# Stationary low parts in four pieces at hashed positions, one load buffer less

## The chip, the cores and the metric

The kernel runs on one core of one Trainium2 chip. The metric is the time of one execution on the device in microseconds (us). A core has TensorE (matmuls, PE in the profile, with its weight loads as PEld), VectorE (DVE), ScalarE (ACT), GpSimd (POOL) and SyncE (SP, which issues most transfers), each with its own queue that is worked off in order, and 128 partitions of on-chip memory.

## The reference

A decoder trunk of two layers on 256 tokens with 2048 channels, all in float32. The first layer is a Mamba-2 mixer, the second attends to keys and values that are computed once from the stream after the first layer. After each mixer stands a gated MLP with a short causal convolution, and after each of the four sub-layers a layer norm of the weighted residual:

```python
for layer in range(DEPTH):
    if layer < N_A_LAYERS:
        mix = mamba2_mixer(h, ...)
    else:
        mix = moba_cross_attention(h, attn_w_q[j], attn_w_o[j], k_blk, v_blk, k_mean)
    h = layer_norm(DEEPNORM_ALPHA * h + mix, ln_mix_g[layer], ln_mix_b[layer])
    ffn = conv_ffn(h, ffn_w_up[layer], ffn_conv_w[layer], ffn_conv_b[layer], ffn_w_down[layer])
    h = layer_norm(DEEPNORM_ALPHA * h + ffn, ln_ffn_g[layer], ln_ffn_b[layer])
```

Nearly all the work lies in the products with the weights: `mamba_w_in`, `mamba_w_out`, `ffn_w_up`, `ffn_w_down`, `w_kv`, `attn_w_q`, `attn_w_o`, some 462 MB as they are cut (881 x 128 x 1024 x 4 bytes).

## The kernel before

A float32 number is written as a high part, rounded to the type float32r that TensorE takes, and a low part, the rest. A product of two numbers is then high x high + low x high + high x low. The activations of a sub-layer lie in on-chip memory once, high and low side by side, with the 2048 channels in 16 blocks k of 128: `hT[:, k, 0, :]` and `hT[:, k, 1, :]`, 256 tokens each (`gT`, `yT` and `aT` in the same form).

The weights are cut into 881 steps of 128 partitions x 1024 numbers (`chunks`, `cut`). For each step `load` issues one transfer of 512 KB into a buffer `raw` on SP's queue; `split` lets ScalarE copy it to `hi` in the type float32r (L209) and VectorE write `lo` = raw - hi (L210), and calls `load` for a step further on. `raw` has `RAW` buffers, `hi` and `lo` have four each, and `splits` keeps the splits up to four steps ahead of the products. A transfer waits on SP until its buffer is free, that is until the subtraction that read it last is done, and everything behind it on SP's queue waits with it: the parts of x and the small columns at the start, the residuals and gains of the norms (`fetch`, `fetch_gb`).

There are two kinds of product. In the 560 steps of mode "W" the weights are stationary and the activations moving; a step holds four blocks k of 256 output channels, thus 8 stationary blocks of 128 x 128 in `hi` and 8 in `lo`. `some` (called by `whole`) multiplies those of `hi` with both parts of the activations, 512 columns (L266), and those of `lo` with the high part, 256 columns (L269). The order of parts alternates, so that `hi` and `lo` stand in runs: in most mamba chunks runs of 16 matmuls of each kind, in the other chunks ("paired", two steps at a time) runs of 32. In the 320 steps of mode "X" the activations are stationary and the weights moving, six matmuls of 512 columns for each half of the tokens (`half`, L231, L232, L236); the last steps of the last chunk of a down projection do the second half in two pieces of 256 columns, into `tp` or `acc`.

Where `lo` lies is set by hand. In a line of 256 bytes (`LINE` is 64 numbers) the activations, `raw` and `hi` all begin at the same place. A tile `gap` of 48 numbers stands between `hi` and `lo`. In a W step the two halves of `lo` begin at the start of the tile and 8.5 lines on; in an X step `lo` begins 16 numbers into it:

```python
l = wts.tile([P, 2 * NC + LINE], F32R, tag="lo", name="lo")
if steps[i][0].mode == "W":
    l = l.rearrange("p (a n) -> p a n", a=2)[:, :, :NC]
else:
    l = l[:, LINE // 4:LINE // 4 + 2 * NC].rearrange("p (a n) -> p a n", a=2)
```

Counted from the beginning of the activations, a W step's low halves thus lie at 192 and 64 bytes in a line, and an X step's low part at 0.

The order of everything else (convolutions, the scan, attention, norms) is written out by hand against step numbers with `at`, `amid`, `within` and `beyond`.

Of the kernel before, what the change touches and what calls it, by code (L numbers as in the profile page):

```python
# [18 lines left out]
F32 = mybir.dt.float32  # L19
F32R = mybir.dt.float32r  # L20
# [4 lines left out]
P = 128  # L25
D = 2048
S = 256
# [12 lines left out]
NC = 512  # L40
HC = NC // 2
NEG = -1.0e30
LINE = 64
# [6 lines left out]
    N_COL += _n // P  # L50

LA = 3
RAW = 4
WARM0 = 18
HEAD, TAIL = 3, 4
LAST = 8
# [3 lines left out]
def chunks():  # L60

    z, b, c, dt = 0, 2 * DI, 2 * DI + NG * DS, 2 * DI + 2 * NG * DS

    def some(mode, name, layer, c0, n, nk):
        return [(mode, name, layer, c0 + i * NC, nk, False) for i in range(n)]

    def ffn(layer):
        up = [some(m, "ffn_w_up", layer, c + j * NC, 1, KD)[0] for j in range(DFF // NC)
              for m, c in (("W" if j else "X", 0), ("W", DFF))]
        return up + some("X", "ffn_w_down", layer, 0, 4, KF)  # L70

    out = some("W", "mamba_w_in", 0, b, 2, KD)
    out[0] = out[0][:5] + (True,)
    out += some("H", "mamba_w_in", 0, dt, 1, KD) + some("W", "mamba_w_in", 0, c, 2, KD)
    for g in range(NG):
        out += some("W", "mamba_w_in", 0, DI + g * NC, 1, KD) + some("W", "mamba_w_in", 0, z + g * NC, 1, KD)
    out += some("X", "mamba_w_out", 0, 0, 4, DI // P) + ffn(0)
    out += some("X", "w_kv", None, D, 1, KD) + some("W", "w_kv", None, 0, 4, KD) + some("W", "attn_w_q", 0, 0, 4, KD)
    return out + some("X", "w_kv", None, D + NC, 3, KD) + some("X", "attn_w_o", 0, 0, 4, KD) + ffn(1)
# [12 lines left out]
def yoco_kernel(ctx: ExitStack, tc: tile.TileContext, x, lmg, lmb, lfg, lfb, x_t, columns, w, out):  # L92
    nc = tc.nc
    base = ctx.enter_context(tc.tile_pool(name="base", bufs=1))
    wts = ctx.enter_context(tc.tile_pool(name="wts", bufs=LA + 1))
# [30 lines left out]
    steps, plan = [], chunks()  # L126
# [39 lines left out]
    raw_t, hi_t, lo_t = {}, {}, {}  # L166
# [5 lines left out]
    def load():  # L172
        i = pos["load"]
        if i >= n_steps:
            return
        pos["load"] += 1
        t = wts.tile([P, 2, NC], F32, tag="raw", name="raw", bufs=RAW)
        for e in (slice(0, 1), slice(1, 2)) if i == 0 else (slice(0, 2),):
            nc.sync.dma_start(t[:, e], w[i][:, e])
        raw_t[i] = t  # L180

    def split():
        i = pos["split"]
        pos["split"] += 1
        t = raw_t.pop(i)
        if i in spare:
            h, l = (bufs["h"][:, k:k + 2].rearrange("p k a t -> p k (a t)") for k in (spare[i], spare[i] + 2))
        else:
            h = wts.tile([P, 2, NC], F32R, tag="hi", name="hi")
            if not gap:  # L190
                gap.append(wts.tile([P, LINE * 3 // 4], F32R, tag="gap", name="gap", bufs=1))
            l = wts.tile([P, 2 * NC + LINE], F32R, tag="lo", name="lo")
            if len(gap) < 2:
                gap.append(wts.tile([P, LINE // 4], F32R, tag="gap2", name="gap2", bufs=1))
            if steps[i][0].mode == "W":
                l = l.rearrange("p (a n) -> p a n", a=2)[:, :, :NC]
            else:
                l = l[:, LINE // 4:LINE // 4 + 2 * NC].rearrange("p (a n) -> p a n", a=2)
        hi_t[i], lo_t[i] = h, l
        if steps[i][0].mode == "H":  # L200
            for a, w in enumerate((h, l)):
                v = t[:, a].rearrange("p (k n) -> p k n", k=8)
                w = w.rearrange("p a (k e n) -> p (a k) e n", e=2, n=NC // 8)
                nc.scalar.copy(w[:, :, 0], v)
                nc.vector.tensor_sub(w[:, :, 1], v, w[:, :, 0].bitcast(F32))
            return load()
        for e in ((0,), (1,)) if i < 2 else ((0, 1),):
            sl = slice(e[0], e[-1] + 1)
            nc.scalar.copy(h[:, sl], t[:, sl])  # L209
            nc.vector.tensor_sub(l[:, sl], t[:, sl], h[:, sl].bitcast(F32))  # L210
        load()

    def splits(i, most=2):

        for _ in range(1 if steps[i][0] in calm else most):
            j = pos["split"]
            ahead = LA + 1 + sum(i <= k < j for k in spare)
            if j < min(i + ahead, n_steps) and (j in spare or sum(k not in spare for k in hi_t) < LA + 1):
                split()
# [30 lines left out]
    def some(ch, s, p):  # L250

        i = ch.first + s
        nj = ch.nj
        w = ((hi_t, lo_t)[p][i]).rearrange("p a (k n) -> p a k n", n=nj * P)
        k0, half = ch.place(s)
        banks = [p[:, j, :] for p in ch.part[half:] for j in range(2)]
        first = ch.kinds(s)[0] == p
        for kk in range(ch.per):
            k = k0 + kk
            a, b = divmod(kk, ch.per // 2)  # L260
            begins, ends = first and k == 0, not first and k == ch.nk - 1
            for j in range(nj):
                yield
                js = slice(j * P, (j + 1) * P)
                if p == 0:
                    nc.tensor.matmul(banks[j], w[:, a, b, js], ch.x.both(k), start=begins, stop=ends,  # L266
                                     skip_group_check=True)
                else:
                    nc.tensor.matmul(banks[j][:, :S], w[:, a, b, js], ch.x.hi(k), start=begins, stop=ends,  # L269
                                     skip_group_check=True)  # L270

    def beside(i):
# [10 lines left out]
    def whole(i):  # L283

        ch, s = steps[i]
        if ch.mode == "H":
            return beside(i)
        a, b = ch.kinds(s)
        if not ch.paired:
            order = [(s, a), (s, b)]  # L290
        elif s % 2 == 0:
            order = [(s, a), (s + 1, a)]
        else:
            order = [(s - 1, b), (s, b)]
        late = ch.paired and s % 2
        n = len(order) * ch.per * ch.nj
        c = 0
        for t, p in order:
            for _ in some(ch, t, p):
                if c == (n // 2 if late else n * 3 // 8):  # L300
                    if late:
                        done(i - 1)
                    run(mid, i)
                    splits(i)
                c += 1
        if not ch.paired or late:
            done(i)
# [821 lines left out]
    for h in range(HEADS):  # L1129
        i, j = divmod(h, 4)  # L1130
# [87 lines left out]
```

## Time and profile before

| | |
|---|---|
| median of 2 runs | 2523.05 us (2522.97 to 2523.14) |
| the profiled execution | 2522.57 us |
| its span, first to last instruction | 2520.3 us |
| granted TensorE clock | 0.999 |
| ScalarE busy | 1365.8 us (54%) |
| VectorE busy | 1658.3 us (66%) |
| transfers of weights from issue to landing, median | 3.9 us |
| HBM read | 491.77 MB, 198 GB/s over the span with what is written |

The lines of the profile name the engine, the line of the program, the operation, what is written and read with the tiles' names, and how often; then busy time in us and the mean of one in ns, and the idle time of the engine before them with what ended it. In the timeline a row has the start and the length in us, and a count where neighbours are merged. A matmul's length there is its latency; successive matmuls overlap, so that the distance of starts is their pace.

### The profile page before, as it was taken

The page shows a single profiled execution, that of the slowest core. Times are in us where ns is not written, and L with a number is a line of the kernel's source. Part 1 is how long each engine was busy: PE and PEld are TensorE (multiplying, and loading weights), DVE is VectorE, ACT ScalarE, POOL GpSimd, SP SyncE. Part 2 cuts the span into 40 slices and gives each one's busy share as a digit, 9 for nine tenths or more (in the row PEclk, how much of TensorE's full clock was granted, in tenths as well). Part 3 has the DMA queues.
Part 4 walks back from the last instruction along what each step waited for, and adds up shares of the span by engine and source line. Part 5 has one row for each costly group of instructions (what it writes and reads, how often), then busy time and mean ns, then how long its engine had stood idle before and what let it go on. Part 6 is the DMA issues. An engine that isn't in the chain of part 4 may idle for free.

```text
span 2520.3 us, 36085 instructions
## 1 busy us (share of the span) xinstructions
PE 2507.3 (99%) x13983; PEld 2180.6 (87%) x13983; DVE 1658.3 (66%) x2140; ACT 1365.8 (54%) x1790; POOL 76.5 (3%) x96
## 2 busy tenths in 40 slices
PE   9999999999999999999999999999999999999998
PEld 8888888888888888888888888888888888888887
DVE  7878878755666766676445646645767676765545
ACT  6677787643465555554333445543556555554333
POOL 0000000000200000000000200000200000000001
PEclk9999999999999999999999999999999999999999
DMA  7656665666665565556676665456655665566674
GB/s 258 206 188 199 210 193 187 198 208 225 207 209 188 193 192 190 193 187 203 203 233 204 210 197 170 160 179 225 222 192 195 193 192 195 184 197 207 196 227 162
DMA packets 141739, 502.59 MB, mean 199 GB/s; under 512 B 15856, under 2 KB 16368, under 8 KB 141568
## 3 DMA queue, kind: packets, MB, share of 16 engines
q1 hardware_dynamic: 136448, 482.92, 58.9%
q0 software_dynamic: 4832, 16.85, 2.1%
q8 instruction: 109, 1.79, 0.3%
q14 instruction: 62, 0.51, 0.1%
q10 hardware_dynamic: 288, 0.52, 0.1%
HBM read 491.77 MB, written 8.45 MB: 198 GB/s over the span
## 4 chain that ended last, share of the span: by engine, by line
PE 99%; DMA 0%; DVE 0%; SPq 0%; issue 0%; ACT 0%
PE acc L266 40%; PE acc L269 21%; PE acc L231 11%; PE acc L232 11%; PE acc L236 11%; PE acc L804 1%; PE tp L406 0%; PE tp L236 0%; PE tp L232 0%; PE tp L231 0%; PE tp L813 0%; PE acc L787 0%; PE tp L1083 0%; PE tp L1117 0%; DMA raw<-in_w 0%; PE tp L1109 0%
## 5 line engine op out<-in xcount | busy, mean ns | idle before, releaser
L210 DVE TENSOR_TENSOR lo<-raw,hi 128x1024 fp32r<-128x1024 f32 (+1 forms) x869 | 1060.0, 1225 | 728.1 <-ACT hi L209 601.3
L209 ACT CAST hi<-raw 128x1024 fp32r<-128x1024 f32 (+1 forms) x869 | 908.9, 1048 | 833.1 <-PE acc L236 367.0
L266 PE MATMUL acc<-hT,hi 128*128 128x512 f32 x4480 | 1058.3, 391 | 1.4 <-DVE hT L569 1.2
L266 PEld LDWEIGHTS acc<-hT,hi 128*128 128x128 f32 x4480 | 826.4, 188 | 165.9 <-ACT hi L209 1.8
L269 PEld LDWEIGHTS acc<-hT,lo 128*128 128x128 f32 x4480 | 548.5, 188 | 15.5 <-issue 1.2
L269 PE MATMUL acc<-hT,lo 128*128 128x256 f32 x4480 | 555.0, 279 | 0.0
L232 PE MATMUL acc<-lo,gT 128*128 128x512 f32 (+1 forms) x678 | 254.5, 378 | 0.0
L231 PE MATMUL acc<-hi,gT 128*128 128x512 f32 (+1 forms) x678 | 254.1, 377 | 0.0
L236 PE MATMUL acc<-hi,gT 128*128 128x512 f32 (+1 forms) x678 | 200.8, 377 | 0.0
L232 PEld LDWEIGHTS acc<-lo,gT 128*128 128x128 f32 x678 | 127.6, 188 | 23.4
L231 PEld LDWEIGHTS acc<-hi,gT 128*128 128x128 f32 x678 | 127.6, 188 | 23.1
L236 PEld LDWEIGHTS acc<-hi,gT 128*128 128x128 f32 x678 | 124.9, 188 | 23.6
L232 PE MATMUL acc<-lo,yT 128*128 128x512 f32 (+1 forms) x270 | 98.6, 369 | 0.0
L231 PE MATMUL acc<-hi,yT 128*128 128x512 f32 (+1 forms) x270 | 98.5, 369 | 0.0
L231 PE MATMUL acc<-hi,hT 128*128 128x512 f32 x192 | 78.7, 410 | 0.0
L236 PE MATMUL acc<-hi,yT 128*128 128x512 f32 (+1 forms) x270 | 77.6, 369 | 0.0
L232 PE MATMUL acc<-lo,hT 128*128 128x512 f32 x192 | 75.4, 393 | 0.0
L636 DVE SCALAR_TENSOR_TENSOR g<-u,cols,g 128x254 f32<-128x254 f32 (+1 forms) x176 | 73.3, 478 | 2.8 <-ACT g L631 2.8
L609 DVE TENSOR_TENSOR u<-u,acc 128x512 f32<-128x512 f32 x108 | 73.5, 681 | 2.3 <-ACT u L608 1.4
L1033 ACT CAST gT<-v 128x512 fp32r<-128x512 f32 x44 | 27.3, 620 | 84.5 <-DVE v L1032 84.5
L636 DVE SCALAR_TENSOR_TENSOR v<-u,cols,v 128x254 f32<-128x254 f32 (+1 forms) x176 | 73.0, 477 | 0.0
L468 POOL TENSOR_TENSOR rs<-rs,mhalf 128x1 f32<-128x1 f32 x8 | 7.4, 931 | 1988.3 <-DVE nb L469 1988.3
(223 smaller groups left out, 1911.2 us busy)
## 6 DMA issues: line engine op xcount, KB each, us to landing
raw<-in_w SPq DMA_DIRECT2D x880, 512.0 KB, 3.9
mA<-acum_d POOLq DMA_DIRECT2D x16, 512.0 KB, 6.4
hres<-r POOLq DMA_DIRECT2D x12, 512.0 KB, 6.7
r<-hres SPq DMA_DIRECT2D x12, 512.0 KB, 4.4
eA<-acum_d POOLq DMA_DIRECT2D x16, 128.0 KB, 7.7
r<-in_x SPq DMA_DIRECT2D x4, 512.0 KB, 5.1
gb<-in_ln_mix_g SPq DMA_DIRECT2D x8, 256.0 KB, 5.3
gb<-in_ln_mix_b SPq DMA_DIRECT2D x8, 256.0 KB, 5.6
```

The source lines that it names most:

```text
L209: nc.scalar.copy(h[:, sl], t[:, sl])
L210: nc.vector.tensor_sub(l[:, sl], t[:, sl], h[:, sl].bitcast(F32))
L231: nc.tensor.matmul(a, th, h[:, kk, sl], start=k == 0, stop=False)
L232: nc.tensor.matmul(a, th, l[:, kk, sl], start=False, stop=False)
L236: nc.tensor.matmul(a, ch.x.lo(k)[:, ts], h[:, kk, sl], start=False, stop=k == ch.nk - 1)
L266: nc.tensor.matmul(banks[j], w[:, a, b, js], ch.x.both(k), start=begins, stop=ends, skip_group_check=True)
L269: nc.tensor.matmul(banks[j][:, :S], w[:, a, b, js], ch.x.hi(k), start=begins, stop=ends, skip_group_check=True)
L468: nc.gpsimd.tensor_tensor(self.rs[:, h, :], self.rs[:, h, :], mhalf[:, 0, :], op=OP.pow)
L609: nc.vector.tensor_add(dst, dst, p[:, :, :S])
L636: nc.vector.scalar_tensor_tensor(d, u[:, i % 2, :S - k], c1(self.at_w, w[n - 1 - k] + self.ia + i), d, op0=OP.mult, op1=OP.add)
L804: nc.tensor.matmul(ps[64 * q:64 * q + 64, c, j * P:(j + 1) * P], G[g]["xdt"][:, c, h * 64:(h + 1) * 64], G[g]["A", c][:, h, :], start=True ...
L1033: nc.scalar.copy(h, v[:, sl])
```

## The change

`RAW` goes from 4 to 3. The tile of `lo` grows from 2 x 512 + 64 to 2 x 512 + 320 numbers, four buffers of it by 4096 bytes in all, which is what one buffer `raw` held. In a W step `lo` is no longer two halves of 512 but four pieces of 256. The first begins 0, 16, 32 or 48 numbers into the tile, the second follows the first with 0, 16, 32 or 48 numbers between, and the second pair follows the first pair at a distance that again moves it by one of four places in the line; which of the 64 combinations is taken comes from a hash of the step's number. VectorE's subtraction writes the four pieces in one instruction, and `some` finds a stationary block by its piece and its place in it. X steps, `hi`, and the numbers and order of all instructions stay.

```diff
-RAW = 4
+RAW = 3
@@ split
-            l = wts.tile([P, 2 * NC + LINE], F32R, tag="lo", name="lo")
+            l = wts.tile([P, 2 * NC + 5 * LINE], F32R, tag="lo", name="lo")
+            ch, s = steps[i]
...
-            if steps[i][0].mode == "W":
-                l = l.rearrange("p (a n) -> p a n", a=2)[:, :, :NC]
+            if ch.mode == "W":
+                o, d, e = (LINE // 4 * ((i * 2654435761 >> 9) // 4 ** m % 4) for m in range(3))
+                e += HC
+                d += 2 * NC // 2
+                while d < 2 * e:
+                    d += LINE
+                if o + 2 * d > 2 * NC + 5 * LINE:
+                    d -= LINE // 4
+                l = l[:, o:o + 2 * d].rearrange("p (a n) -> p a n", a=2)[:, :, :2 * e]
+                l = l.rearrange("p a (b n) -> p a b n", b=2)[:, :, :, :HC]
             else:
                 l = l[:, LINE // 4:LINE // 4 + 2 * NC].rearrange("p (a n) -> p a n", a=2)
...
-            nc.vector.tensor_sub(l[:, sl], t[:, sl], h[:, sl].bitcast(F32))
+            if len(l.shape) == 4:
+                u, v = (y[:, sl].rearrange("p a (b n) -> p a b n", b=2) for y in (t, h.bitcast(F32)))
+                nc.vector.tensor_sub(l[:, sl], u, v)
+            else:
+                nc.vector.tensor_sub(l[:, sl], t[:, sl], h[:, sl].bitcast(F32))
@@ some
-        w = ((hi_t, lo_t)[p][i]).rearrange("p a (k n) -> p a k n", n=nj * P)
+        w = (hi_t, lo_t)[p][i]
+        if len(w.shape) == 3:
+            w = w.rearrange("p a (b n) -> p a b n", b=2)
...
-                js = slice(j * P, (j + 1) * P)
+                c, j0 = divmod(b * nj * P + j * P, HC)
+                js = slice(j0, j0 + P)
...
-                    nc.tensor.matmul(banks[j][:, :S], w[:, a, b, js], ch.x.hi(k), start=begins, stop=ends,
+                    nc.tensor.matmul(banks[j][:, :S], w[:, a, c, js], ch.x.hi(k), start=begins, stop=ends,
                                      skip_group_check=True)
```

More of the change, by code (lines that the diff above doesn't have):

```diff
@@ L263, in some @@
                 yield
-                js = slice(j * P, (j + 1) * P)
+                c, j0 = divmod(b * nj * P + j * P, HC)
+                js = slice(j0, j0 + P)
                 if p == 0:
-                    nc.tensor.matmul(banks[j], w[:, a, b, js], ch.x.both(k), start=begins, stop=ends,
+                    nc.tensor.matmul(banks[j], w[:, a, c, js], ch.x.both(k), start=begins, stop=ends,
                                      skip_group_check=True)
                 else:
-                    nc.tensor.matmul(banks[j][:, :S], w[:, a, b, js], ch.x.hi(k), start=begins, stop=ends,
+                    nc.tensor.matmul(banks[j][:, :S], w[:, a, c, js], ch.x.hi(k), start=begins, stop=ends,
                                      skip_group_check=True)
```

## The prediction

> **What bounds the kernel now.** I read the page first: the shares of the engines, the slices and the chain.
>
> ```profile
> span 2520.3 us, 36085 instructions
> ...
> PE 2507.3 (99%) x13983; PEld 2180.6 (87%) x13983; DVE 1658.3 (66%) x2140; ACT 1365.8 (54%) x1790; POOL 76.5 (3%) x96
> ...
> PEclk9999999999999999999999999999999999999999
> ...
> PE 99%; DMA 0%; DVE 0%; SPq 0%; issue 0%; ACT 0%
> PE acc L266 40%; PE acc L269 21%; PE acc L231 11%; PE acc L232 11%; PE acc L236 11%; PE acc L804 1%; PE tp L406 0%; PE tp L236 0%; PE tp L232 0%; PE tp L231 0%; PE tp L813 0%; PE acc L787 0%; PE tp L1083 0%; PE tp L1117 0%; DMA raw<-in_w 0%; PE tp L1109 0%
> ```
>
> TensorE is the chain from end to end, at an even, full clock. No other engine can give time back; what counts is the pace of one matmul after another, and whether something new makes TensorE wait. The change touches the stationary operand of L269, so next the groups by line, shapes kept apart:
>
> ```profile
> L266 PE MATMUL acc<-hT,hi 128*128 128x512 f32 x4480 | 1058.3, 391 | 1.4 <-DVE hT L569 1.2 <-ACT hi L209 0.2
> L210 DVE TENSOR_TENSOR lo<-raw,hi 128x1024 fp32r<-128x1024 f32 x865 | 1057.4, 1227 | 727.5 <-ACT hi L209 600.7 <-ACT v L631 67.7 <-ACT g L631 33.7
> L209 ACT CAST hi<-raw 128x1024 fp32r<-128x1024 f32 x865 | 906.5, 1050 | 832.4 <-PE acc L236 367.0 <-PE acc L266 279.1 <-issue 101.7
> L269 PE MATMUL acc<-hT,lo 128*128 128x256 f32 x4480 | 555.0, 279 | 0.0
> L875 DVE TENSOR_TENSOR yT<-y,yT 128x1024 fp32r<-128x1024 f32 x8 | 9.7, 1218 | 0.0
> ```
>
> The 279 ns is one matmul's latency; they overlap, so the pace must be had from whole groups. L269 runs in unbroken groups: by the chunk list 8 in the first chunk, 4 in each of 19 other mamba chunks, 2 in each of 50 paired chunks, 184 in all. A group of n lasts (n-1) paces and one 279 ns, so the pace is (555.0 - 184 x 0.279) / (4480 - 184) = 117.2 ns. It isn't the same everywhere. The timeline of TensorE around one paired group of the first FFN, and then at the end of the last down projection, where 256-column matmuls have gT as stationary and hi or lo as moving operand:
>
> ```profile
> 809.35 3.86 PE L269 MATMUL acc<-hT,lo 128*128 128x256 f32 x32
> 813.04 4.27 PE L266 MATMUL acc<-hT,hi 128*128 128x512 f32 x18
> ```
>
> ```profile
> 809.35 2.04 PE L269 MATMUL acc<-hT,lo 128*128 128x256 f32 x16
> ```
>
> ```profile
> 2498.92 0.28 PE L231 MATMUL tp<-hi,gT 128*128 128x256 f32 x1
> 2499.04 0.28 PE L232 MATMUL tp<-lo,gT 128*128 128x256 f32 x1
> 2499.16 0.28 PE L236 MATMUL tp<-hi,gT 128*128 128x256 f32 x1
> ```
>
> The first 16 of the paired group go at (2.04 - 0.28) / 15 = 117.3 ns. All 32 take 813.04 - 809.35 = 3.69 us, so the other 16 take 3.69 - 16 x 0.1173 = 1.81, or 113.3 each. In the last fence the starts lie 120 ns apart. L266, with twice the columns, goes at (4.27 - 0.39) / 17 = 228 ns; half of it is 114. So 113.3 is about what 256 columns cost, and 4 to 7 ns above it come and go between matmuls of one shape. That excess is all that the change can win or lose on TensorE.
>
> **The change part by part.**
>
> *Positions of the low parts.* In a W step lo now lies as two halves, at 192 and 64 bytes in a 256-byte line as counted from hi and the activations (gap of 48 elements, then a half of 8.5 lines). In the tail the stationary gT and the moving hi and lo all sit at 0. So the trace shows 120 ns for equal positions, and 113.3 to 117.3 for 192 and 64. After the change each of the four pieces of 256 lies at 0, 64, 128 or 192. Running the hash over the 560 W steps gives 560 pieces at 0, 554 at 64, 556 at 128, 570 at 192, and only a third of the steps have none at 0. Nothing shows position 128, nor 64 beside 192 in one half. Bounds: all at 113.3 gives 4480 x -3.9 ns = -17.5 us; all at 120 gives 4480 x 2.8 = +12.5 us. I take 120 for the quarter at 0, to which the tail is nearest, and 117.2 for the rest: 0.25 x 2.8 x 4480 = +3.1 us.
>
> The page TensorE: Matmul & The Clock Gate of the Trainium skill, section Step-by-step: what each phase is for, gives TensorE "two independent read ports", one for the moving and one for the stationary operand. By that no position of lo could matter and this term would be 0. The trace has three paces for one shape, which that sentence alone doesn't explain. Its section LDWEIGHTS (loading the stationary operand) puts a load at columns / 1.2, an estimate of 107 ns here, so hidden under 113; no row shows that price by itself.
>
> *The subtraction.* L210 writes four pieces where it wrote two, with the same count. L875 writes four pieces of 256 at a stride already: 1218 ns against 1227. So 560 x 0, hidden by VectorE's idle 727.5 us before L210 anyway; without that cover 560 x 0.009 would be 5 us of gain. Matmuls, weight loads and ACT copies keep number and shape.
>
> *One load buffer less.* Load j+4 goes out when split j is done; now it waits for split j+1, about one step later. The waits, and the loads:
>
> ```profile
> SPq L179 <- DVE lo L210: 1884.5, 819, 5.2
> ```
>
> ```profile
> ACT hi L209 <- PE acc L236: 367.0, 221, 4.7
> ACT hi L209 <- PE acc L266: 279.1, 238, 5.7
> ACT hi L209 <- DMA raw<-in_w: 36.0, 28, 3.7
> ```
>
> ```profile
> raw<-in_w SPq DMA_DIRECT2D x880, 512.0 KB, 3.9
> ```
>
> Copies wait for TensorE to free a hi tile 459 times, for a load 28 times. A buffer is taken for 3.9 us of load, 1.05 of copy and 1.23 of subtraction, 6.2 in all; three of them pass a step each 2.1 us, and a W step lasts 8 x (0.228 + 0.117) = 2.76 us. So on average loads keep up, and hi and lo stay four deep. It bites where loads come in bursts or queue behind others: start, three norms, end.
>
> ```profile
> 19.14 0.33 SPq L179 DMA_DIRECT2D raw<-in_w  x1
> 19.52 0.42 SPq L119 DMA_DIRECT2D cols<-in_columns  x1
> ```
>
> ```profile
> 19.63 1.22 DVE L210 TENSOR_TENSOR lo<-raw,hi 128x1024 fp32r<-128x1024 f32 x1
> ...
> 30.53 3.74 DVE L210 TENSOR_TENSOR lo<-raw,hi 128x1024 fp32r<-128x1024 f32 x3 [2.84 <-ACT hi L209]
> ...
> 31.35 2.05 PE L269 MATMUL acc<-hT,lo 128*128 128x256 f32 x16
> ```
>
> Start: load 8 goes at 19.14 and would go at 20.85, when the subtraction at 19.63 ends; behind it on SP's queue stand the columns and load 9, 1.7 us late each at most. Step 9 has its low part at 30.53 + 1.23 = 31.76 and TensorE takes it after eight matmuls of step 8, at 32.29: 0.5 us to spare, 1.2 lost. (The last part of x queues behind load 3 in the same way; it is used five steps on.)
>
> ```profile
> 2490.21 2.35 DVE L210 TENSOR_TENSOR hT<-raw,hT 128x1024 fp32r<-128x1024 f32 x2
> ...
> 2496.02 1.23 DVE L210 TENSOR_TENSOR hT<-raw,hT 128x1024 fp32r<-128x1024 f32 x1 [1.89 <-ACT hT L209]
> ```
>
> ```profile
> 2487.50 3.15 SPq L179 DMA_DIRECT2D raw<-in_w  x2
> 2490.70 0.42 SPq L439 DMA_DIRECT2D r<-hres  x1
> ```
>
> ```profile
> 2497.56 0.39 PE L232 MATMUL acc<-hT,gT 128*128 128x512 f32 x1
> ```
>
> End: the last load leaves by 2490.65; it would wait for the first of the two subtractions, 2491.4, so it and the residual and gain loads behind it come 1.1 us later. The last low part, ready at 2497.25, is read at 2497.56: 0.8 lost.
>
> ```profile
> 693.65 1.05 ACT L209 CAST hi<-raw 128x1024 fp32r<-128x1024 f32 x1 [3.28 <-DMA raw<-in_w]
> ...
> 695.09 3.79 PE L266 MATMUL acc<-hT,hi 128*128 128x512 f32 x16
> ```
>
> Norms: here a copy waits 3.28 us for its load and ends at 694.70; TensorE needs that hi at 695.09 + 8 x 0.228 = 696.9, 2.2 us on, which hides a delay of 1 to 2. ScalarE's queue stands behind the waiting copy, so some of it can leak: 0.5 us for each of three norms. Sum of the buffer: 1.2 + 0.8 + 1.5 = 3.5 us. Bounds: 0, if loads with fewer in flight land that much sooner; and a full step of 2.76 at each of five places, 14 us.
>
> **Sum.** 3.1 + 0 + 3.5 = +6.6 us. The profiled span is 2520.3, its execution took 2522.57 with 2.3 us around the span, and the median of the two runs is 2523.05; the sum goes on that: **2529.7 us**.
>
> **Rivals.**
> - *New positions free the loads.* For it: 16 matmuls in a row did run at 113.3 with positions 192 and 64 in turn, so the excess isn't a must. Against: a quarter of the pieces lands where the tail shows 120. In full 2523.05 - 17.5 + 3.5 = 2509; half of it 2518. Faster than before. Chance 0.25.
> - *Every change of position breaks the good state.* The 113.3 comes only in the second half of long groups; with a new position every two matmuls it may never come, and all go at 120: 2523.05 + 12.5 + 3.5 = 2539. Slower; it decides once the mean pace is over 118. Chance 0.18.
> - *Positions do nothing*, the excess is a start-up of each group, as the order in the paired group could also be read. Only the buffer stays: 2526.5. Chance 0.12. The sentence of the Trainium skill on two read ports (TensorE: Matmul & The Clock Gate) would have it so.
> - *The loads starve TensorE*: 14 us in place of 3.5, 2540, from the point where a wait of SP exceeds the 2.2 us of cover at the norms. For it: the copy at 693.65 waits 3.28 us for its load already, and those behind it would too. Chance 0.05.
> - *Something that no row shows*, beyond 2%: 0.03 slower, 0.01 faster.
>
> **How the numbers follow.** The forecast has the remaining 0.36 and runs from 2522 to 2538; the third rival lies within it. Both signs are held by more than a tenth, slower by about three quarters. The range takes in the second rival with a few us more for the buffer, and the first down to its greater part: 2511 to 2545. Faster by over 2% would be under 2472.6, slower over 2573.5 (2% is about what a measurement of this kernel can tell from no change). The streaming pace leaves 17.5 us to win, 0.7%, so faster has 0.01; slower needs a pace of 128 ns, above any shown, 0.03; the rest 0.96.
>
> **What would show it.** The L269 group's busy sum, by the formula above: 117.9 ns right, under 115 the first rival, 119 or more the second, 117.2 the third. Within a paired group, starts by pairs of matmuls: pairs at position 0 at 120, others less. L210 at 1227 again, or the four pieces cost after all. Copies that wait for a load: from 28 times to some hundred, with no new idle time of PE but a us or so near 32, 690, 1420, 1805 and 2497; several us there mean starvation. L266 at 1058 us, or the stationary low parts act on the high ones too. The forecast is wrong as a whole if positions move the pace by more than 3 ns either way.

## The result

The changed kernel takes 2548.55 us (median of 2 runs, 2545.68 to 2551.42) against 2523.05, a ratio of 1.0102 with a 95% interval of 1.0085 to 1.0119. It is slower by 25.5 us. The forecast was 6.6 us slower, and its range ended at 2545, so the time lies outside it: the direction was right, the size was not.

### The profile after

The profiled execution took 2551.42 us, 28.85 over the one of before. Its page (in the changed kernel L266 is L282, L269 is L285; L210 is L221 for W steps and L223 for the others; L209 is L218):

```profile
span 2549.3 us, 36083 instructions
...
PE 2522.0 (99%) x13983; PEld 2191.7 (86%) x13983; DVE 1658.2 (65%) x2140; ACT 1367.6 (54%) x1790; POOL 76.0 (3%) x96
...
PE 84%; DMA 6%; DVE 5%; ACT 3%; issue 2%; POOL 0%; SPq 0%; ACTq 0%; DVEq 0%; POOLq 0%
...
L282 PE MATMUL acc<-hT,hi 128*128 128x512 f32 x4480 | 1060.0, 391 | 1.2 <-DVE hT L585 0.8
...
L221 DVE TENSOR_TENSOR lo<-raw,hi 128x1024 fp32r<-128x1024 f32 (+1 forms) x562 | 681.6, 1219 | 410.3 <-ACT hi L218 297.8
...
L285 PE MATMUL acc<-hT,lo 128*128 128x256 f32 x4480 | 562.5, 281 | 0.4 <-DVE lo L221 0.4
```

The chain of waits was 99% TensorE; now it is 84%, and the rest runs through the loads, the subtraction and the copy. The reader should not take TensorE's 99% busy for health: it is counted from modelled ends, and the chain shows the change. By the prediction's formula the pace of L285 is (562.5 - 184 x 0.281) / 4296 = 118.9 ns, before 117.2: 1.7 ns on 4480 matmuls is 7.6 us. The formula's 184 unbroken groups are too few: in the trace of before L269 runs in 199, 92 of them of 32 matmuls. Taken from start to start inside the groups, without the 20 to 30 gaps over 200 ns, the pace is 116.2 ns before and 117.7 after, a difference of 1.5 ns or 6.7 us. All paces by the formula below are about 1 ns too high in the same way, so they compare well with one another, but not with single gaps. The waits of the changed kernel (total us, times, longest):

```profile
ACT hi L218 <- DMA raw<-in_w: 167.3, 147, 4.2
...
PE tp L422 <- POOL r L512: 5.1, 3, 2.2
```

Copies wait for their load 147 times, 28 before, and TensorE's transposes in the norms wait.

Where the time went is seen best by setting each of the 13983 matmuls of a trace against the same one of before, and taking how much further behind it has fallen at the end of each stretch. This table is worked out so from the starts in the traces; the stretches are in us of the trace of before, and each row is one execution:

```
us lost in       0-130 130-560 640-720 720- 1385- 1440- 1760- 1840- 2480-   sum
                 start  heads  norm 1  1385  1440  1760  1840  2480   end
                                       FFN 1 nrm 2 att.  nrm 3 FFN 2
changed kernel    0.79   7.83   2.88   2.81  3.68  0.87  5.48  2.69  1.97  29.00
e1  3 buffers     1.13   4.22   1.62   0.00  1.23  0.09  5.05  0.00  1.47  14.80
e2  positions     0.54   0.85   0.15   3.34  0.06  1.15  0.31  3.28  0.00   9.69
e5  e1, gains     1.31   7.51   2.89   0.00  0.58  0.00  3.95  0.00  1.58  17.80
e6  e1, late mean 2.62  12.93   2.04   0.00  1.27  0.09  3.83  0.00  1.31  24.09
e7  e1, both      1.43  10.15   3.67   0.00 -0.01  0.09  6.19  0.00  2.30  23.82
e9  4th in heads -0.33   0.01   1.15   0.00  1.45  0.09  3.77  0.00  1.39   7.52
e10 4th at norms  2.97   3.73   0.03   0.00  0.02  0.05 -0.07  0.00  1.35   8.09
e11 e1, no bcast  0.96   0.00   2.04   0.00  3.51  0.09  5.15  0.00  1.62  13.37
e12 4, no bcast  -0.59   0.00  -0.08   0.00  0.01  0.00 -0.11  0.00  1.01   0.24
e16 quarters     -0.71  -3.19  -0.11  -2.40 -0.05 -0.97 -0.31 -2.34  0.00 -10.09
```

(560 to 640 us, the output projection, is nothing in every row and left out.) The first row has two kinds of loss: a smooth one in the FFN and attention stretches, and larger ones in the head groups of the mixer, at the three norms and at the end. Some 4.7 of the first row's 29.00 us are neither pace nor waiting: TensorE's granted clock falls to half behind three of the stalls (the last section shows it). The second and third rows, explained below, separate the two kinds.

One of the stalls in the head groups, in the changed kernel's timeline:

```profile
369.43 1.05 ACT L218 CAST hi<-raw 128x1024 fp32r<-128x1024 f32 x1 [1.71 <-DMA raw<-in_w]
370.38 0.40 ACT L857 CAST sq<-sz 128x256 fp32r<-128x256 f32 x1
...
371.66 0.42 DVE L858 TENSOR_TENSOR sq<-sz,sq 128x256 fp32r<-128x256 f32 x1
...
372.13 0.39 PE L864 MATMUL tp<-sq,mean 128*128 128x256 f32 x1 [0.91 <-DVE sq L858]
```

A copy waits 1.71 us for its load. The rounding of the squares stands behind it on ScalarE, their low part behind the weights' on VectorE, and TensorE stands for 0.91 us before the mean of the squares.

### The profile page after: what moved, and what is told of

The parts are those of the page before. It is cut to its first block, busy times and chain, and to the rows that moved or that the text cites. A ratio compares the mean times of both kernels' runs of the same rounds, so it can differ in the third digit from the quotient of the medians.

```text
span 2549.3 us, 36083 instructions
## 1 busy us (share of the span) xinstructions
PE 2522.0 (99%) x13983; PEld 2191.7 (86%) x13983; DVE 1658.2 (65%) x2140; ACT 1367.6 (54%) x1790; POOL 76.0 (3%) x96
## 4 chain that ended last, share of the span: by engine, by line
PE 84%; DMA 6%; DVE 5%; ACT 3%; issue 2%; POOL 0%; SPq 0%; ACTq 0%; DVEq 0%; POOLq 0%
PE acc L282 32%; PE acc L285 16%; PE acc L245 11%; PE acc L244 11%; PE acc L249 11%; DMA raw<-in_w 5%; DVE lo L221 2%; ACT hi L218 1%; PE tp L422 0%; PE tp L249 0%; PE tp L245 0%; PE tp L244 0%; ACT mA L768 0%; DVE xc L652 0%; DVE mA L787 0%
## 5 line engine op out<-in xcount | busy, mean ns | idle before, releaser
L218 ACT CAST hi<-raw 128x1024 fp32r<-128x1024 f32 (+1 forms) x869 | 909.2, 1049 | 888.7 <-PE acc L249 355.8
L282 PE MATMUL acc<-hT,hi 128*128 128x512 f32 x4480 | 1060.0, 391 | 1.2 <-DVE hT L585 0.8
L282 PEld LDWEIGHTS acc<-hT,hi 128*128 128x128 f32 x4480 | 827.8, 188 | 165.9 <-ACT hi L218 1.6
L221 DVE TENSOR_TENSOR lo<-raw,hi 128x1024 fp32r<-128x1024 f32 (+1 forms) x562 | 681.6, 1219 | 410.3 <-ACT hi L218 297.8
L223 DVE TENSOR_TENSOR lo<-raw,hi 128x1024 fp32r<-128x1024 f32 x307 | 378.2, 1233 | 350.4 <-ACT hi L218 344.7
L285 PEld LDWEIGHTS acc<-hT,lo 128*128 128x128 f32 x4480 | 555.1, 189 | 16.6 <-issue 0.9
L285 PE MATMUL acc<-hT,lo 128*128 128x256 f32 x4480 | 562.5, 281 | 0.4 <-DVE lo L221 0.4
```

The source lines that it names most:

```text
L221: nc.vector.tensor_sub(l[:, sl], u, v)
L282: nc.tensor.matmul(banks[j], w[:, a, c, js], ch.x.both(k), start=begins, stop=ends, skip_group_check=True)
L285: nc.tensor.matmul(banks[j][:, :S], w[:, a, c, js], ch.x.hi(k), start=begins, stop=ends, skip_group_check=True)
```

## The experiments

The kernel before ran beside each group of runs, with medians of 2522.6 to 2523.1. Times are medians of 3 to 8 runs.

### The two parts apart: e1 to e4

e1 is the kernel before with one load buffer less; `lo` stays as it was.

```diff
-RAW = 4
+RAW = 3
```

> Only one load buffer less; the low parts lie as before. Theory A (the buffer costs most: waits for loads and for what stands behind them on SP's queue): 2538 to 2544 us, L269 at 555 us busy as before, and TensorE stops at the same places as in the changed kernel (before the norms' transposes, before the sum of squares of the mamba groups, at the last two steps). Theory B (the positions cost most, the buffer only the 3.5 us of the prediction): 2526 to 2528 us. Theory C (neither alone, only both together): under 2530 us, and the next kernel under 2526 us too.

2540.0 us, ratio 1.0074 (1.0057 to 1.0090), with L269 at 555.3 us, as theory A has it. The buffer alone costs 17.0 us. Its four executions lie between 2537.24 and 2545.46 us; the one traced is the fastest.

e2 keeps four buffers and gives the low parts a mix of positions that fits into the old tile: nine layouts in place of 64, chosen by the same hash.

```diff
+FITS = [(0, 0, 0), (1, 0, 0), (2, 0, 0), (3, 0, 0), (0, 1, 0), (1, 1, 0), (2, 1, 0), (0, 2, 0), (0, 2, 1)]
...
+                o, d, e = FITS[(i * 2654435761 >> 9) % len(FITS)]
+                o, d, e = o * LINE // 4, NC + d * LINE // 4, HC + e * LINE // 4
```

> Only the positions, with four load buffers: per step one of nine layouts that fit the old tile, by the same hash, all four positions in use (9, 9, 11 and 7 of 36 pieces at 192, 0, 64 and 128). Theory A: 5 to 9 us over before, 2528 to 2532 us, the low matmuls' group at 560 to 564 us busy, copies that wait for a load about 28 times as before. Theory B: 2540 us or more. Theory C: under 2526 us.

2532.28 us, ratio 1.0037 (1.0024 to 1.0050): 9.3 us, 0.3 over the end of theory A's range; copies wait for a load 28 times, as before. The two parts make 26.3, the whole change 25.5. Within the spread of the three-buffer runs they add up, though the nine layouts are not the change's 64. In the table their rows fall on different stretches: the positions on FFN and attention, the buffer on the rest.

e3 and e4 put all low parts of the W steps at one position, contiguous, at 0 and at 64 of the 256 bytes.

```diff
-                l = l.rearrange("p (a n) -> p a n", a=2)[:, :, :NC]
+                l = l[:, LINE // 4:LINE // 4 + 2 * NC].rearrange("p (a n) -> p a n", a=2)
```

(e3; e4 has `2 * LINE // 4` in both places.)

> All low stationary blocks at the activations' own position 0, four load buffers. If equal positions clash as the tail of the kernel before was read (120 ns): 2535 us. By the pairs of the changed kernel's trace (118.7 ns where one block at 0 follows another, against 116.7 for all of before): 2530 to 2533 us. If positions do nothing: 2523 us.

> All low stationary blocks at position 64, four load buffers. If it is the position as such that counts, and 64 is as good as 192: 2521 to 2525 us, the same as before. If a run needs the alternation of 192 and 64 to reach 113 ns: 2526 us or more.

e3 took 2540.11 us (1.0052 to 1.0082 of before), e4 2530.11 (1.0017 to 1.0039). Their groups of the low matmuls on the page, in this order e2, e3, e4:

```profile
L281 PE MATMUL acc<-hT,lo 128*128 128x256 f32 x4480 | 563.3, 281 | 0.0
```

```profile
L269 PE MATMUL acc<-hT,lo 128*128 128x256 f32 x4480 | 570.6, 283 | 0.0
```

```profile
L269 PE MATMUL acc<-hT,lo 128*128 128x256 f32 x4480 | 562.1, 281 | 0.0
```

By the formula these are 119.1, 120.7 and 118.8 ns. At 0 the pace is the 120 of the prediction, and the time lies above everything that was expected of e3. But 64 alone is slower than before's halves at 192 and 64 (117.2), as the second expectation of e4 has it.

### What the buffer costs, first theory: e5 to e8

The trace of e1 suggested theory A: the gain and bias loads of a norm's fourth chunk queue on SP behind a weight load that waits for its buffer. SP's timeline of before, and then of e1, near 1405 us (start, length, count; a row of several loads holds their waits):

```profile
1402.40 0.33 SPq L444 DMA_DIRECT2D gb<-in_ln_ffn_g  x1
1402.78 0.43 SPq L444 DMA_DIRECT2D gb<-in_ln_ffn_b  x1
```

```profile
1389.28 25.42 SPq L179 DMA_DIRECT2D raw<-in_w  x7
1414.74 0.42 SPq L444 DMA_DIRECT2D gb<-in_ln_ffn_g  x1
1415.22 0.42 SPq L444 DMA_DIRECT2D gb<-in_ln_ffn_b  x1
```

TensorE is 7 us behind there, the gains 12. e5 issues these two loads from GpSimd; e6 moves the mean of the squares to a step later; e7 is both, on three buffers, and e8 both on the changed kernel.

```diff
-        beyond(n + 1, 0, None, norm.fetch_gb, 3)
+        beyond(n + 1, 0, None, norm.fetch_gb, 3, nc.gpsimd)
```

```diff
-        at(s0 + 23, z_rms, g)
+        at(s0 + 24, z_rms, g)
```

> The kernel before with three load buffers (2540.0 us), and in the three norms inside the kernel the gain and bias loads of the fourth chunk issued by GpSimd and not by SyncE, so that they no longer stand behind a weight load that waits for its buffer. Theory A (the norms stall because these small loads queue behind that waiting load): the stalls of 0.3 to 2.5 us in front of the norms' transposes, 7.5 us in all, go, and the time comes to about 2532; SyncE's weight loads wait as before. Rival (the norms stall because ScalarE's queue stands behind a copy that waits for its load, as the prediction had it): the stalls stay, about 2540.

> The kernel before with three load buffers (2540.0 us), and the mean over the squares on TensorE (z_rms) one step later, in step s0 + 24 in place of s0 + 23. Theory A (the copy for the sum of squares stands on ScalarE behind a copy that waits for its load, and TensorE had only 0.5 us in hand there): the four stalls of 0.4 to 1.2 us, 3.7 us in all, go: about 2536. Rival (the delay is more than a step, or moves on to the logarithm and the scaling behind it): 2540 or more.

> Both edits on three load buffers. Theory A: the savings add up, 7.5 and 3.7 us off 2540.0: about 2529, and what is left over 2523 is the stall of the last two steps (1.4 us), the clock after long stalls and small waits. Rival (a missing buffer costs in many places at once and the time comes back elsewhere): 2535 to 2540.

> The changed kernel (2548.55 us: low parts at 64 combinations of positions, three buffers) with the same two edits. Theory A (the buffer's 17 us are those two places, and the positions' 9 us are apart from it): the positions' loss stays and most of the buffer's goes, 2533 to 2537. Rival (with the spread positions the stalls come from TensorE's changed pace, not from the queue): 2545 or more.

None came as theory A expected: 2540.97 (2536.65 to 2544.42), 2546.08, 2546.87 and 2552.30 us. The times of e5, e6 and e8 are those of their rivals; e7 lies above both of its ranges. In e5 the gains do leave some 5 us sooner, counted from TensorE's delay, and three stalls are gone from the trace that e1 has inside the norms, where TensorE waits 1.4 to 1.5 us for GpSimd's last operation with the gains (L496) and falls 1.6 us further behind each time. But other stalls at the norms took their place, 1.2 us at the first and 2.7 at the third the largest; the norms lose 7.4 us by the table, 7.9 in e1. (The heads, where e1 and e5 are the same, lose 4.2 and 7.5 us: single executions with three buffers differ by some us.) The queue on SP is real, and taking it away alone doesn't bring the time down.

e6 got rid of the stalls before the mean too, and lost more. The logarithm stayed in its step, had to wait there on ScalarE for the mean, and held up the copies behind it. The waits of e6 from 130 to 560 us, and the row of L269:

```profile
ACT sz L852 <- DVE sz L849: 6.9, 8, 1.1
```

```profile
L269 PE MATMUL acc<-hT,lo 128*128 128x256 f32 x4480 | 559.1, 279 | 10.3 <-DVE lo L210 10.3
```

ScalarE waits 6.9 us for the logarithm's input, in e1 not at all, and TensorE 10.3 us for low parts. So e6 shows only that this consumer can't be moved alone; as a test of what delays the splits it is inconclusive. Theory A fell: both edits were made where the delay arrives, and it arrived elsewhere.

### Where the buffer is missed: e9 to e12

Theory D says that the loss is a sum over places at which the splits (copy and subtraction) must run faster than one a step, or a load lands late, and the copies have no fourth load lying ready. e9 and e10 give back the fourth buffer in one kind of place.

```diff
+        if i % 4 == 3 and steps[i][0].name[:5] == "mamba":
+            t = wts.tile([P, 2, NC], F32, tag="raw4", name="raw", bufs=1)
+        else:
+            t = wts.tile([P, 2, NC], F32, tag="raw", name="raw", bufs=RAW)
```

(e9, with `name` kept in the chunk; e10 has the condition `any(e - 12 <= i < e + 16 for e in edges())`, with the steps at which the stage changes after `mamba_w_out`, `ffn_w_down` and `attn_w_o`.)

> Three load buffers and, for the weights of the first stage alone (the names that begin with mamba, to about 650 us), a fourth one that takes every fourth load. The traces of the three-buffer kernels put their loss against before in four places: the head-group stage (30 to 560 us) 4.8 to 8.4 us, the three inner norms 7.1 to 7.9 us, the first steps 0.5 us, the last ones 1.5 us. Theory D (the loss is a sum over these places, in each of which the splits run ahead in a burst or a load is late, and the missing buffer shows as a wait there): the first stage's part goes and the norms' stays, 2532 to 2536 (2540.0 with three). Rival (the loss sits in the norms, and what the first stage loses is made up or moves on): 2538 or more.

> Three load buffers, and the fourth for the loads around the three inner norms alone (from 12 steps before to 16 after the change of stage). Theory D: the norms' 7 to 8 us go and the first stage's stay, 2530 to 2534. Rival (the loss sits in the first stage, or the norms' stall has another cause than the buffer): 2538 or more.

2532.30 (2529.97 to 2534.37) and 2532.62 us (2530.50 to 2535.41), 7.7 and 7.4 less than with three buffers. The table shows the same by place: with the fourth buffer in the first stage the heads lose 0.01 us, with one at the norms these lose 0.03, 0.02 and -0.07. The first stage of e9 takes in the start, which loses nothing there either (-0.33). The 17 us are therefore about 7.7 in the first stage with the start, 7.4 at the norms and 2 at the end.

What is late at the third norm can be read from ScalarE and VectorE. Ahead of a norm ScalarE makes the copies of seven splits as fast as their loads come. Before, near the third norm:

```profile
1762.40 1.05 ACT L209 CAST hi<-raw 128x1024 fp32r<-128x1024 f32 x1 [3.10 <-PE acc L236]
1763.35 3.02 ACT L209 CAST hT<-raw 128x1024 fp32r<-128x1024 f32 x3
1768.23 1.05 ACT L209 CAST hi<-raw 128x1024 fp32r<-128x1024 f32 x1 [1.86 <-DMA raw<-in_w]
1770.71 1.05 ACT L209 CAST hi<-raw 128x1024 fp32r<-128x1024 f32 x1 [1.43 <-DMA raw<-in_w]
1772.09 1.05 ACT L209 CAST hi<-raw 128x1024 fp32r<-128x1024 f32 x1 [0.33 <-DMA raw<-in_w]
1778.47 0.82 ACT L491 ACTIVATE r<-r,nb,rs 128x512 f32<-128x512 f32 x1 [5.33 <-POOL nb L470]
```

and in e1:

```profile
1770.68 1.05 ACT L209 CAST hi<-raw 128x1024 fp32r<-128x1024 f32 x1 [3.10 <-PE acc L236]
1771.63 1.04 ACT L209 CAST hT<-raw 128x1024 fp32r<-128x1024 f32 x1
1773.53 1.05 ACT L209 CAST hT<-raw 128x1024 fp32r<-128x1024 f32 x1 [0.85 <-DMA raw<-in_w]
1776.22 1.05 ACT L209 CAST hT<-raw 128x1024 fp32r<-128x1024 f32 x1 [1.65 <-DMA raw<-in_w]
1779.53 1.05 ACT L209 CAST hi<-raw 128x1024 fp32r<-128x1024 f32 x1 [2.27 <-DMA raw<-in_w]
1780.86 1.05 ACT L209 CAST hi<-raw 128x1024 fp32r<-128x1024 f32 x1 [0.28 <-DMA raw<-in_w]
1783.50 1.05 ACT L209 CAST hi<-raw 128x1024 fp32r<-128x1024 f32 x1 [1.58 <-DMA raw<-in_w]
1789.22 0.81 ACT L491 ACTIVATE r<-r,nb,rs 128x512 f32<-128x512 f32 x1 [4.68 <-POOL nb L470]
```

Before, four copies run back to back on loads that lie ready; in e1 two. From the first start to the seventh it takes 9.7 us before (1762.40 to 1772.09) and 12.8 in e1. The first copy comes 8.3 us later than before, which is TensorE's delay by then, and L491, the norm's first step on ScalarE, 10.75: 2.5 us have been added. ScalarE itself is free in both cases and waits some 5 us for GpSimd ahead of L491. The norm begins on VectorE, with the sum of residual and product (L450). VectorE before, and then in e1:

```profile
1771.79 2.60 DVE L210 TENSOR_TENSOR lo<-raw,hi 128x1024 fp32r<-128x1024 f32 x2 [1.25 <-ACT hi L209]
1774.94 0.69 DVE L450 SCALAR_TENSOR_TENSOR r<-r,acc 128x512 f32<-128x512 f32 x1 [0.55 <-PE acc L236]
```

```profile
1784.58 1.22 DVE L210 TENSOR_TENSOR lo<-raw,hi 128x1024 fp32r<-128x1024 f32 x1 [1.41 <-ACT hi L209]
1785.72 0.68 DVE L450 SCALAR_TENSOR_TENSOR r<-r,acc 128x512 f32<-128x512 f32 x1
```

Before, L450 waits for TensorE's product; in e1 it stands right behind the subtraction of the seventh split, which the late load has pushed back. TensorE then falls 2.5 us further behind before its first transposes. In e5, with its gains sooner, the seven starts take 13.0 us too.

So the norms' 7.9 us in the trace of e1 have two causes: the three stalls of 1.6 us behind the gains, and these 2.5 us behind the burst, with 1.5 us of half clock after them; the rest is made up again. A fourth buffer takes both away, moving the gains only the first; how the 7.4 us share out between them stays open.

In the head groups another load shares the DMA engines: on GpSimd's queue each group fetches its decay, 1.25 MB. e11 fills those tiles with zeros instead, on three buffers, and e12 does so on four; the decay's values are left out of the computation.

```diff
-            nc.gpsimd.dma_start(t, bass.AP(tensor=s.tensor, offset=s.offset, ap=[[0, P], [S, 8], [1, P]]))
+            nc.gpsimd.memset(t, 0.0)
```

(and the same for `eA`)

> Three load buffers, and the broadcast loads of the decay (mA and eA, 1.25 MB for each head group on GpSimd's queue) left out: the tiles are filled with zeros instead, so the decay's values are not the reference's. Theory F (in the head groups the weight loads land late because the DMA engines are shared with these loads: 4.3 to 8.8 us to landing near 355 us where the median of the whole run is 3.3; a fourth buffer hides that): the first stage's 4.8 to 8.4 us go, 2532 to 2536. Rival G (the loads are late because the buffer is freed late, behind the elementwise work that ScalarE and VectorE do between two splits): 2538 or more.

> The same left out of the kernel before, with its four load buffers: the control. If a fourth buffer hides these loads in full, 2522 to 2524 as before; if the loads cost something there too, less than 2521.

e11 took 2535.37 us (2533.09 to 2542.58), 4.6 less than e1; e12 2522.24, no different from before (0.9987 to 1.0008). The transfers and the waiting copies from 130 to 560 us, in the view by tile, of before, e1 and e11 (us and times that copies waited; shortest, median and longest load):

```profile
  DMA raw<-in_w: 0.5, 1
...
DMA to landing us min/median/max: 3.1/4.1/8.8
```

```profile
  DMA raw<-in_w: 40.4, 32
...
DMA to landing us min/median/max: 3.1/3.8/9.8
```

```profile
  DMA raw<-in_w: 29.1, 23
...
DMA to landing us min/median/max: 3.0/3.4/5.2
```

Loads that take up to 8.8 us exist before, and only one copy in this stretch ever waits for one (0.5 us): the fourth buffer covers them. With three, 32 copies wait 40.4 us. The three largest stalls in the head groups of e1 stand behind such loads. The first:

```profile
308.30 12.57 SPq L179 DMA_DIRECT2D raw<-in_w  x4
```

```profile
318.20 1.05 ACT L209 CAST hi<-raw 128x1024 fp32r<-128x1024 f32 x1 [1.40 <-DMA raw<-in_w]
```

The first load of the row on SP is the one that the copy waits for: it left at 308.30, as soon as its buffer was free, and the copy starts 9.9 us later. At the other two these are 9.6 and 9.5 us. Without the decay's loads the longest takes 5.2 us; the copies still wait 29.1 us, but TensorE loses nothing, 0.00 in the table. So theory F holds for this stage, as far as one trace and a median with a spread of 9 us carry: what it loses is the late loads. The rival, buffers freed late behind elementwise work, may be behind those 29.1 us, which cost nothing. (The time fell by 4.6 us and not by the 7.7 of e9; in the executions traced, the norms of e11 lost 10.7 us by the table, those of e1 7.9.)

### What the pace hangs on: e13 to e16

Four more with four buffers: all at 192 (e13), all at 128 (e14), before's halves exchanged to 64 and 192 (e15), and the eight blocks of a step at 192, 192, 64, 64, 64, 64, 192, 192 (e16). e13 and e14 differ from e3 by the offset, 0 and `3 * LINE // 4`. e15:

```diff
+            if steps[i][0].mode == "W":
+                for a in e:
+                    nc.vector.tensor_sub(l[:, 1 - a], t[:, a], h[:, a].bitcast(F32))
+                continue
...
-                    nc.tensor.matmul(banks[j][:, :S], w[:, a, b, js], ch.x.hi(k), start=begins, stop=ends,
+                    nc.tensor.matmul(banks[j][:, :S], w[:, 1 - a, b, js], ch.x.hi(k), start=begins, stop=ends,
```

e16 leaves the gap of 32 numbers inside a half too, not only between the halves:

```diff
-                l = l.rearrange("p (a n) -> p a n", a=2)[:, :, :NC]
+                l = l.rearrange("p (a n) -> p a n", a=2)
...
+            if steps[i][0].mode == "W":
+                for c in range(2):
+                    y, z = (slice(c * v, c * v + HC) for v in (HC, HC + LINE // 2))
+                    nc.vector.tensor_sub(l[:, sl, z], t[:, sl, y], h[:, sl, y].bitcast(F32))
+                continue
...
-                js = slice(j * P, (j + 1) * P)
+                c = b * nj + j
+                js = slice(c * P + p * c // 2 * (LINE // 2), (c + 1) * P + p * c // 2 * (LINE // 2))
```

> Four load buffers, the stationary low parts of the W steps contiguous, all at 192 of the 256 bytes (before: the first half of a step at 192, the second at 64). Theory S (one position alone stays in the slow pace of about 117.8 ns, as 64 did; the pace of 113.3 is reached where the position changes between the halves): 2528 to 2532. Rival P (192 is the good position, and before's slow matmuls are those at 64): 2512 to 2518.

> The same at 128. Theory S: a slow pace throughout, 2528 to 2533 if 128 is like 64, 2538 to 2541 if it is like 0 (the changed kernel's gaps after blocks at 128 were 118.35 ns, those at 0 118.2, at 64 117.0, at 192 117.3). Rival P: in between, 2528 or less.

> Four load buffers, before's places with the halves exchanged: the first half at 64, the second at 192 (the subtraction in two instructions). Theory S (it is the change of position that settles the pace, in either direction): 2521 to 2525. Rival (only a change from 192 to 64 at a certain place of the group does it): 2526 to 2531.

> Four load buffers, the blocks of a step at 192, 192, 64, 64 and 64, 64, 192, 192 (the subtraction in two instructions): as many changes of position as before, at other places of the group. Theory S: 2515 to 2524, the lower end if the pace settles earlier than after before's 11 matmuls. Rival (only a run of one half at one position lets it settle; a change within the half breaks it, as in the mixes): 2528 to 2533.

e13 took 2534.37 us, e14 2540.40, e15 2520.70 (0.9979 to 1.0001), and e16 2513.12 us, a ratio of 0.9960 (0.9941 to 0.9980): e16 beats both kernels, by 9.9 us the one before. Of theory S's ranges only e14's holds (128 is like 0); e13 lies 2.4 us above its range, e15 0.3 and e16 1.9 below theirs, all on the side away from the rivals. The groups of e13, e14, e15 and e16:

```profile
L269 PE MATMUL acc<-hT,lo 128*128 128x256 f32 x4480 | 562.0, 280 | 0.0
```

```profile
L269 PE MATMUL acc<-hT,lo 128*128 128x256 f32 x4480 | 572.5, 284 | 0.0
```

```profile
L273 PE MATMUL acc<-hT,lo 128*128 128x256 f32 x4480 | 552.7, 279 | 0.0
```

```profile
L275 PE MATMUL acc<-hT,lo 128*128 128x256 f32 x4480 | 544.4, 277 | 0.0
```

Paces of 118.8, 121.1, 116.7 and 114.9 ns. From start to start, as above, they are 117.7, 120.2, 115.6 and 113.7. The pace of e16 accounts for its gain: 2.3 ns on 4480 matmuls is 10.3 us. The pace of the low matmuls does not account for all of e13: it is that of e4, and the time is 4.3 us longer. There the high matmuls are slower, L266 at 1063.1 us against 1058.4 in e4; why is open. The time from start to start within one group of 32 low matmuls in the first FFN, in ns, worked out from the traces:

```
before    117 119 117 119 117 118 117 118 118 117 119 114 117 122 118 114 113 113 114 113 113 114 113 113 114 113 113 ...
e15       118 118 117 123 117 118 118 114 117 123 118 113 114 113 113 114 113 113 114 113 113 114 113 113 114 113 113 ...
e16       118 115 115 113 113 114 113 113 114 113 113 114 113 113 114 113 113 114 113 113 114 113 113 114 113 113 114 ...
e13       117 119 117 118 118 117 118 118 118 117 119 117 118 118 117 118 118 119 116 119 117 118 118 117 119 117 119 ...
e4        118 118 117 118 118 118 117 119 117 118 118 117 118 118 118 117 119 117 118 118 117 118 118 118 117 119 117 ...
changed   124 120 116 114 114 113 119 121 113 118 113 120 113 116 114 113 119 121 113 118 113 118 117 118 118 118 120 ...
```

At one position, 64 or 192, a group stays at 118 to its end. Where positions change between 192 and 64 it settles at 113.3, after 16 matmuls before, after 12 in e15, after 2 to 4 in e16, and so in all 92 groups of 32. In the changed kernel it reaches 113 for a few matmuls and is thrown out again, and blocks at 0 and 128 bring 120 and more. Theory S holds against rival P: no position is fast by itself. Which change settles the pace, and why the first change of before (after its fourth matmul) did not, stays open.

## Why the prediction was wrong

**What bounds the kernel.** Right in that every us came from TensorE, by its pace or a new wait. What it had no term for is TensorE's clock: "even, full" before, it falls to half three times behind the new stalls, some 4.7 us in the execution traced.

**The position term, +3.1 us.** It came out at 7.6 us in the changed kernel's trace by the formula (6.7 from start to start), and e2's mix cost 9.3. The mechanism was half right. The price of 120 holds where all pieces lie at 0 (e3: 120.7). In the changed kernel the start of a matmul on a piece at 0 comes 118.2 ns after the start ahead of it, at 128 118.4, at 192 117.3 and at 64 117.0, against 116.2 on average before: the pieces at 0 cost 2.0 ns each, less than the forecast 2.8, and the other three 0.8 to 2.2, where the forecast had nothing. What failed is "117.2 for the rest": it is the mean of two states of one group, 118 and 113.3, that the prediction itself had read from the timeline, and only some orders of positions reach the lower one. A mix loses that order. (117.2 is itself 1 ns too high, as told above.) The prediction's second rival named this ("with a new position every two matmuls it may never come") and its condition, a mean pace over 118, was met; its price of 12.5 us was too high because not all blocks go at 120. Position 128, which no row showed, is 121.1 alone.

The sentence of the Trainium skill on "two independent read ports" (TensorE: Matmul & The Clock Gate, section Step-by-step: what each phase is for) would have made this term 0. The runs speak against reading it so: the kernel takes 2540.40 us with all low parts at 128 and 2513.12 at quarters of 192 and 64.

**The subtraction, 0.** Right: 1219 ns against 1227. High matmuls are right too, 1060.0 us against 1058.3.

**The buffer term, +3.5 us.** This is the step that failed most: 17.0 us alone. "So on average loads keep up" was true, and beside the point; where they come in bursts, the prediction left out one place and priced another by the wrong cover. The place left out is the head groups, where loads of up to 8.8 us to landing cost nothing before because four buffers covered them, and 7.7 us with three (the start among them). The norms were priced at 0.5 us each, since one copy had 2.2 us until TensorE needed it and only a little would leak through ScalarE's queue. They cost 7.4 us, by other ways: gains that queue on SP behind a waiting load, and a burst of seven splits that grew by 3.1 us at the third norm and held up the norm's first operation on VectorE, where ScalarE was free. Start and end were about right, 1.2 and 0.8 forecast, 1.1 and 1.5 in the trace of e1.

**The rivals and the range.** "The loads starve TensorE" gave 2540, and e1 took 2540.0. That the two agree is chance: the rival's 2540 holds 14 us of buffer and 3.1 of positions, e1 17.0 of buffer alone, 7.7 of it in a place that the rival didn't count. It had a chance of 0.05, and the second rival 0.18, each with the small value of the other term: 2539 or 2540. Both came together. The two terms have nothing to do with one another, so their bad ends belonged in one case of 2523.05 + 12.5 + 14 = 2549.6, and the upper end of the range near it. The first rival, "New positions free the loads", was wrong for these positions, but e16 shows that others do speed up the matmuls.

**What would show it.** The waits rose from 28 to 147, the "some hundred" forecast, and stalls stood near 690, 1420, 1805 and 2497 as named. Those at the norms were several us, which was said to mean starvation; those in the head groups were named nowhere.

## What to carry to other kernels

Judge a buffer by its worst place, not by the mean rate: look for the stretch where no consumer waits although single loads take twice the median, and for bursts that run ahead on purpose, and price the loss of a buffer there, on every queue that the burst shares with other work. When the pace of one shape of instruction has two values within a group, a mean over them is no price for a changed order; ask what carries the group from one to the other. When a delay is found, moving what arrives late is worth little while the producer stays late: giving the buffer back in one place at a time told more than moving the consumers.

## What the runs showed of the hardware

Where the stationary operand lies in a 256-byte line, counted from the moving operand, changes the pace of 256-column float32r matmuls: by the formula 120.7 ns at 0, 121.1 at 128, 118.8 at 64 and at 192, and 114.9 where 192 and 64 alternate by quarters of a step (119.6, 120.2, 117.7, 117.7 and 113.7 from start to start). For these matmuls positions 128 bytes apart thus behave alike. Only the stationary operand was moved, so the runs don't show whether the distance between the operands counts or the place alone.

Behind some stalls of TensorE the granted clock falls to half. In the changed kernel it does so three times, for 3.4 us each. A view of these stretches (the number before the last two is the clock's mean):

```profile
424.90:428.20 3.30, 3.30 (x11) 2.64 (x10) 2.60 (x4) 3.27 (x5) 0.00 (x0) 0.50 0.41 144
1431.80:1435.10 3.30, 3.30 (x12) 2.62 (x11) 3.30 (x5) 1.54 (x3) 2.00 (x6) 0.50 0.99 303
1800.50:1803.80 3.30, 3.30 (x16) 3.30 (x17) 1.33 (x3) 0.77 (x2) 2.55 (x2) 0.50 0.00 0
```

The stalls ahead of them are two of 0.9 us each within 2.2 us, one of 2.2 us and one of 2.4 us. Each such stretch puts TensorE some 1.5 us further behind, so part of what a stall costs comes after it. The trace of before has none between the start and the last steps. The trace of e1 has one, from 1790.0, and that of e5 none, though TensorE stands still for 2.5 us there at the third norm. Which stalls bring it on stays open.
